# A gated encoder block: the recurrence's gate products as 64-row products in the two halves of the array

## The chip, the cores and the metric

The kernel runs on one core of a Trainium2 chip. The metric is the device time of one execution in microseconds (us), as the median of several runs. Profiles come from the hardware profiler; PE is TensorE, PEld its weight loads, DVE VectorE, ACT ScalarE, POOL GpSimd, SP the engine that issues the loads.

## The reference

One layer of a bidirectional encoder over 256 tokens of 1024 features, in fp32. Four mixers (a gated linear recurrence, differential attention, latent attention, retention) read one wide projection of the normalised input, are merged through sigmoid gates, and a feed-forward part follows. The change touches the recurrence alone:

```
xblk = xc.reshape(b, s, LRU_BLOCKS, LRU_BLOCK)        # 16 blocks of 64 features
for d in range(2):                                    # forwards and backwards in time
    r = sigmoid(einsum('bsnc,ncd->bsnd', xblk, wa[d]).reshape(b, s, w) + ba[d])
    i = sigmoid(einsum('bsnc,ncd->bsnd', xblk, wx[d]).reshape(b, s, w) + bx[d])
    log_a = -LRU_C * r * softplus(-lam[d])
    a = exp(log_a)
    u = sqrt(-expm1(2.0 * log_a)) * (i * xc)
    _, h = associative_scan(combine, (a, u), axis=1, reverse=(d == 1))
    h_sum = h_sum + h
return h_sum * gelu(ga)
```

The gates r and i are block-diagonal products: each block of 64 features is multiplied by a 64 × 64 matrix of its own, once for r and once for i, and for each direction d.

## The kernel before

The large products (`acc<-...` in the profile) stream weights from HBM. `load` fetches a tile `raw` of up to 1 MB (three buffers); `pieces` splits it into `hi` and `lo` (five buffers each), of which `hi` is written by ACT or, for some, by DVE, and `lo` by DVE; PE then makes three products in fp32r per piece. In `b_mode` 24 products of 256 columns use one piece, in `a_mode` 12 of up to 512.

The mixers run beside that stream as generators: `tick` after each weight tile advances those in the list `side`, by a credit that `pace` sets, and `finish` drains them. A scheduler then orders the instructions of each engine; every engine runs its own list in order. Nothing waits by time, only on semaphores. Loads of weights are given a higher priority than what stands around them.

The recurrence is made of 4 units u of 256 features. `a_in(u)` makes `xc`, with features on partitions: half f holds 128 features, that is two blocks of 64. `a_mix(u, xc, rr)` then makes the gates. Its weights come packed by `_pack_lru`: for each f, gate y and direction d a 128 × 128 matrix `bd` that holds two 64 × 64 blocks on its diagonal and zeros elsewhere. For each d there are four fp32 products of 128 rows (2 gates × 2 halves f), each with 256 columns (tokens), into two PSUM tiles `mm` (one per gate). ACT applies the sigmoid with the bias from the columns of `par` and writes `rr` (the r gate) and `ii` (the i gate). Later steps read them: ACT makes `aa` with Exp and Tanh of `rr`, DVE multiplies `ii` by `xc`, and a scan follows. `a_out(u)` needs the result, after the b mixer's projections.

On SP, the loads of `raw` and `bd` stand in one queue in order. POOL makes only the rsqrt steps (two instructions on a tile of a few columns each: `brs`, `bss`, `csc` and the like), whose readers are on DVE. Small tiles such as `rr`, `ii`, `aa`, `bd` and the copies `bx` of the b mixer are taken in turn from a pool `SH` of 16 buffers, so a new tile waits until the buffer's last reader is done.

Of the kernel before, what the change touches and what calls it, by code (L numbers as in the profile page):

```python
# [10 lines left out]
AF = mybir.ActivationFunctionType  # L11
# [62 lines left out]
def _pack_weights(w):  # L74
# [4 lines left out]
    for o, (name, r0, rows, n0, nn, mode) in offs.values():  # L79
# [3 lines left out]
        else:  # L83
# [2 lines left out]
    return flat  # L86


_COLS = (('norm1_g', 8), ('conv_w', 32), ('conv_b', 8), ('lru_ba', 16), ('lru_bx', 16),
         ('mla_qa_g', 3), ('mla_kva_g', 2), ('norm2_g', 8), ('norm3_g', 8), ('diff_sub_g', 1),  # L90
         ('ret_gn_g', 1), ('mla_q_g', 1), ('mla_k_g', 1), ('diff_q_g', 1), ('diff_k_g', 1),
         ('lru_lambda', 16))
# [11 lines left out]
def _pack_params(w):  # L104

    import numpy as np

    out = np.empty((P, N_PAR), np.float32)
    for name, k in _COLS:
        v = np.asarray(w[name][0])  # L110
        if name in ('diff_q_g', 'diff_k_g'):
            v = np.concatenate([np.ones(16, np.float32), v[16:]] * 2)
        elif name in ('mla_q_g', 'mla_k_g'):
            v = v[:P]
        out[:, _COL[name]:_COL[name] + k] = v.reshape(k, P).T
    rows = []
    for dn, mn in (('diff_q_g', 'mla_q_g'), ('diff_k_g', 'mla_k_g')):
        d, m = np.asarray(w[dn][0])[:16], np.asarray(w[mn][0])[P:]
        rows += [d, m, d[8:], d[:8], m[32:], m[:32]]
    rows.append(np.asarray(w['diff_lam'][0]).reshape(-1))  # L120
    out[:, O_GR:O_ROPE] = np.concatenate(rows)[None, :]
    out[:, O_ROPE:] = _rope().reshape(2, P, 288).transpose(1, 0, 2).reshape(P, 576)
    return out


def _pack_lru(w):

    import numpy as np

    out = np.zeros((4, 2, P, 2, 2, P), np.float32)  # L130
    for y, name in enumerate(('lru_wa', 'lru_wx')):
        v = np.asarray(w[name][0]).reshape(2, 4, 2, 2, 64, 64)
        for e in range(2):
            out[:, :, 64 * e:64 * e + 64, y, :, 64 * e:64 * e + 64] = v[:, :, :, e].transpose(1, 0, 3, 2, 4)
    return out


# [30 lines left out]
def encoder_kernel(ctx: ExitStack, tc: tile.TileContext, a, out):  # L168
# [17 lines left out]
    def mm_bank():  # L186
        return psmm.tile([P, 512], F32, tag="mm", name="mm")
# [7 lines left out]
    def act(o, x, f, **kw):  # L195
        nc.scalar.activation(o, x, f, **kw)  # L196

    def mm(o, lhsT, rhs, start, stop):
        nc.tensor.matmul(o, lhsT=lhsT, rhs=rhs, start=start, stop=stop)  # L199
# [246 lines left out]
    with tc.tile_pool(name="br", bufs=1) as br:  # L446
# [4 lines left out]
        def SH(name):  # L451
            return br.tile([P, 512], F32, tag="SH", name=name, bufs=NS)
# [66 lines left out]
        def a_mix(u, xc, rr):  # L519

            R, I, A = [], [], []
            bds = []
            for d in range(2):
                bd = SH("bd")
                nc.sync.dma_start(bd, a['lru'][u, d].rearrange("p y f n -> p (y f n)"))
                bds.append(bd.rearrange("p (y f n) -> p y f n", y=2, n=P))
            yield 0.1
            for d in range(2):
                bd = bds[d]
                R.append(rr if d == 0 else SH("rr").rearrange("p (f s) -> p f s", s=S))  # L530
                I.append(SH("ii").rearrange("p (f s) -> p f s", s=S))
                for y, (dst, bn) in enumerate(((R[d], 'lru_ba'), (I[d], 'lru_bx'))):
                    ps = mm_bank().rearrange("p (f s) -> p f s", s=S)
                    for f in range(2):
                        mm(ps[:, f, :], bd[:, y, f, :], xc[:, f, :], True, True)
                    for f in range(2):
                        act(dst[:, f, :], ps[:, f, :], AF.Sigmoid, bias=c1(bn, 8 * d + 2 * u + f))
                yield 1.5
            for d in range(2):
                A.append(SH("aa").rearrange("p (f s) -> p f s", s=S))  # L540
                aa, r_, i_ = A[d], R[d], I[d]
                for f in range(2):
                    c = 8 * d + 2 * u + f
                    act(aa[:, f, :], r_[:, f, :], AF.Exp, scale=sp[:, 1, c:c + 1])
                    act(r_[:, f, :], r_[:, f, :], AF.Tanh, scale=sp[:, 0, c:c + 1])
                sq = SH("sq").rearrange("p (f s) -> p f s", s=S)
                act(sq, aa, AF.Square)
                stt(r_, sq, 1.0, r_, ADD, MULT)
                tt(i_, i_, xc, MULT)
                yield 2.1  # L550
            for d in range(2):
                aa, r_, i_ = A[d], R[d], I[d]
                act(r_, r_, AF.Sqrt, bias=eps[:, 1:2])
                tt(i_, i_, r_, MULT)
                first = 0 if d == 0 else S - 1
                nc.vector.memset(aa[:, :, first:first + 1], 0.0)
                ao, uo, ho = (x.rearrange("p f s -> p (f s)") for x in (aa, i_, r_))
                if d == 1:
                    ao, uo, ho = ao[:, ::-1], uo[:, ::-1], ho[:, ::-1]
                nc.vector.tensor_tensor_scan(out=ho, data0=ao, data1=uo, initial=0.0, op0=MULT, op1=ADD)  # L560
                yield 1.8
            tt(R[0], R[0], R[1], ADD)
            yield 0.6
# [533 lines left out]
```

## Time and profile before

| what | value |
|---|---|
| three timed runs | 733.2, 734.09, 734.31 us; median 734.09 |
| the profiled execution | 732.92 us |
| its span | 731.1 us |
| granted clock of TensorE | full (1.0) |
| first and last gate product | 30.8 and 104.6 us from the span's start |
| DMA, mean over the span | 176 GB/s |

The span is the time between the first and the last instruction that the profiler saw. A timeline's row gives the start, the duration, the engine, the line, the operation, out<-in with partitions × elements, how many instructions were merged, and in square brackets how long the engine sat idle before and what released it. Durations of products overlap, since PE is pipelined: their cost is read from one start to the next. An fp32 product shows as two records. A row of the view of windows has the busy time of PE, PEld, DVE, ACT and POOL in this order, each with a count. In the views of DMAs, the last number is the median time from issue to landing.

### The profile page before, as it was taken

The page shows a single profiled execution, that of the slowest core. Times are in us where ns is not written, and L with a number is a line of the kernel's source. Part 1 is how long each engine was busy: PE and PEld are TensorE (multiplying, and loading weights), DVE is VectorE, ACT ScalarE, POOL GpSimd, SP SyncE. Part 2 cuts the span into 40 slices and gives each one's busy share as a digit, 9 for nine tenths or more (in the row PEclk, how much of TensorE's full clock was granted, in tenths as well). Part 3 has the DMA queues.
Part 4 walks back from the last instruction along what each step waited for, and adds up shares of the span by engine and source line. Part 5 has one row for each costly group of instructions (what it writes and reads, how often), then busy time and mean ns, then how long its engine had stood idle before and what let it go on. Part 6 is the DMA issues. An engine that isn't in the chain of part 4 may idle for free.

```text
span 731.1 us, 10616 instructions
## 1 busy us (share of the span) xinstructions
PE 714.7 (98%) x4066; PEld 622.6 (85%) x4066; DVE 526.2 (72%) x893; ACT 427.7 (58%) x744; POOL 49.3 (7%) x58
## 2 busy tenths in 40 slices
PE   5999999999999999999999999999999999999997
PEld 4988889997888898888888888878899999888886
DVE  5988978998777879976775788576666666446652
ACT  7589867483755996556654443545755555445551
POOL 0000012222011033110000101000000000000000
PEclk9999999999999999999999999999999999999999
DMA  8754544365344254444545475553565555636611
GB/s 312 260 212 173 172 173 145 114 248 182 134 162 137 91 177 169 173 159 144 179 166 217 138 256 197 191 184 143 177 225 176 173 177 185 215 118 229 233 53 58
DMA packets 22802, 128.47 MB, mean 176 GB/s; under 512 B 2656, under 2 KB 2912, under 8 KB 9440
## 3 DMA queue, kind: packets, MB, share of 16 engines
q1 hardware_dynamic: 22752, 127.80, 49.8%
q8 instruction: 32, 0.52, 0.3%
q14 instruction: 18, 0.15, 0.1%
HBM read 126.74 MB, written 1.05 MB: 175 GB/s over the span
## 4 chain that ended last, share of the span: by engine, by line
PE 64%; DVE 1%; ACT 0%; issue 0%
PE acc L199 57%; PE mm L199 3%; PE mm L212 2%; PE mm L203 1%; ACT hi L196 0%; DVE lo L190 0%; DVE gate L193 0%; DVE pg L190 0%; DVE y L193 0%; DVE xs L190 0%; ACT pg L196 0%
## 5 line engine op out<-in xcount | busy, mean ns | idle before, releaser
L190 DVE TENSOR_TENSOR lo<-raw,hi 128x1024 fp32r<-128x1024 f32 (+3 forms) x226 | 268.2, 1192 | 116.6 <-ACT hi L196 116.0
L196 ACT ACTIVATE hi<-raw 128x1024 fp32r<-128x1024 f32 (+2 forms) x200 | 207.7, 1043 | 192.6 <-PE acc L199 161.2
L199 PE MATMUL acc<-hi,xTh 128*128 128x512 f32 (+3 forms) x376 | 146.3, 389 | 0.0
L199 PE MATMUL acc<-hi,xTl 128*128 128x512 f32 (+3 forms) x376 | 142.8, 380 | 0.0
L199 PE MATMUL acc<-lo,xTh 128*128 128x512 f32 (+3 forms) x376 | 142.5, 379 | 0.0
L199 PE MATMUL acc<-hi,y 128*128 128x512 f32 x448 | 142.1, 393 | 0.0
L199 PE MATMUL acc<-xTl,hi 128*128 128x256 f32 x384 | 109.2, 285 | 0.2 <-DVE xTl L193 0.2
L199 PE MATMUL acc<-xTh,hi 128*128 128x256 f32 x384 | 109.2, 286 | 0.0
L199 PE MATMUL acc<-xTh,lo 128*128 128x256 f32 x384 | 108.7, 284 | 0.0
L199 PEld LDWEIGHTS acc<-hi,y 128*128 128x128 f32 x448 | 84.1, 188 | 17.5
L199 PE MATMUL acc<-lo,y 128*128 128x512 f32 x224 | 87.8, 392 | 0.0
L199 PEld LDWEIGHTS acc<-hi,xTl 128*128 128x128 f32 x376 | 70.6, 188 | 13.2
L199 PEld LDWEIGHTS acc<-hi,xTh 128*128 128x128 f32 x376 | 70.7, 188 | 12.9
L199 PEld LDWEIGHTS acc<-lo,xTh 128*128 128x128 f32 x376 | 70.8, 188 | 12.2
L199 PEld LDWEIGHTS acc<-xTl,hi 128*128 128x128 f32 x384 | 74.1, 193 | 0.7 <-DVE xTl L193 0.6
L199 PEld LDWEIGHTS acc<-xTh,hi 128*128 128x128 f32 x384 | 73.9, 193 | 0.1
L199 PEld LDWEIGHTS acc<-xTh,lo 128*128 128x128 f32 x384 | 73.8, 193 | 0.1
L199 PEld LDWEIGHTS acc<-lo,y 128*128 128x128 f32 x224 | 42.1, 188 | 8.3
L199 PE MATMUL acc<-hi,h 128*128 128x512 f32 x128 | 40.8, 398 | 0.0
L199 PEld LDWEIGHTS acc<-hi,h 128*128 128x128 f32 x128 | 24.0, 188 | 5.7
L199 PE MATMUL acc<-lo,h 128*128 128x512 f32 x64 | 25.3, 396 | 0.0
L199 PE MATMUL acc<-hi,cT 128*128 128x384 f32 (+1 forms) x80 | 24.2, 369 | 0.8 <-ACT cqp L196 0.8
(225 smaller groups left out, 889.9 us busy)
## 6 DMA issues: line engine op xcount, KB each, us to landing
raw<-in_weights_dram SPq DMA_DIRECT2D x104, 1024.0 KB, 4.8
raw<-in_weights_dram SPq DMA_DIRECT2D x6, 512.0 KB, 3.5
raw<-in_weights_dram SPq DMA_DIRECT2D x4, 576.0 KB, 3.8
bd<-in_lru_dram SPq DMA_DIRECT2D x8, 256.0 KB, 5.3
gb<-in_gate_b_dram SPq DMA_DIRECT2D x8, 256.0 KB, 5.2
dec<-in_decay_dram SPq DMA_DIRECT2D x8, 256.0 KB, 6.2
raw<-in_weights_dram SPq DMA_DIRECT2D x2, 768.0 KB, 4.3
raw<-in_weights_dram SPq DMA_DIRECT2D x2, 640.0 KB, 3.7
```

What stands on the lines that cost most here:

```text
L190: nc.vector.tensor_tensor(out=o, in0=x, in1=y, op=op)
L196: nc.scalar.activation(o, x, f, **kw)
L199: nc.tensor.matmul(o, lhsT=lhsT, rhs=rhs, start=start, stop=stop)
L203: nc.tensor.matmul(o, lhsT=lhsT, rhs=rhs, start=start, stop=stop, skip_group_check=True)
L212: nc.tensor.transpose(o, x, ident[:x.shape[0], :x.shape[0]])
```

## The change

Each gate product of 128 rows becomes two of 64 rows. `_pack_lru` no longer writes block-diagonal matrices with zeros: for each block of 64 features it puts the r matrix in columns 0 to 63 and the i matrix in columns 64 to 127. Block e = 0 lies on partitions 0 to 63 and e = 1 on partitions 64 to 127, each with its own PSUM tile, so the products of one half f use the upper and the lower half of the array in turn. The number of products is the same: 4 per direction and unit. The weights of both directions now fit one tile `bd` of 256 KB; before there were two.

After the sigmoids, the tile `g[0]` holds r of block 0 on partitions 0 to 63 and i of block 0 on partitions 64 to 127; `g[1]` (named `gx`) holds the same of block 1. Three DMAs on POOL's queue put the halves where the rest of the code reads them. The biases are packed to match.

```
-_COLS = (('norm1_g', 8), ('conv_w', 32), ('conv_b', 8), ('lru_ba', 16), ('lru_bx', 16),
+_COLS = (('norm1_g', 8), ('conv_w', 32), ('conv_b', 8), ('lru_b', 32),
...
+        if name == 'lru_b':
+            v = np.concatenate([np.asarray(w[n][0]).reshape(32, 64) for n in ('lru_ba', 'lru_bx')], axis=1)
...
-    out = np.zeros((4, 2, P, 2, 2, P), np.float32)
+    out = np.zeros((4, P, 2, 2, P), np.float32)
...
-            out[:, :, 64 * e:64 * e + 64, y, :, 64 * e:64 * e + 64] = v[:, :, :, e].transpose(1, 0, 3, 2, 4)
+            out[:, 64 * e:64 * e + 64, :, :, 64 * y:64 * y + 64] = v[:, :, :, e].transpose(1, 3, 0, 2, 4)
...
         def a_mix(u, xc, rr):
             R, I, A = [], [], []
-            bds = []
+            bd = SH("bd")
+            nc.sync.dma_start(bd, a['lru'][u].rearrange("p d f n -> p (d f n)"))
+            bd = bd.rearrange("p (d f n) -> p d f n", d=2, n=P)
+            yield 0.1
             for d in range(2):
-                bd = SH("bd")
-                nc.sync.dma_start(bd, a['lru'][u, d].rearrange("p y f n -> p (y f n)"))
-                bds.append(bd.rearrange("p (y f n) -> p y f n", y=2, n=P))
-            yield 0.1
-            for d in range(2):
-                bd = bds[d]
-                R.append(rr if d == 0 else SH("rr").rearrange("p (f s) -> p f s", s=S))
-                I.append(SH("ii").rearrange("p (f s) -> p f s", s=S))
-                for y, (dst, bn) in enumerate(((R[d], 'lru_ba'), (I[d], 'lru_bx'))):
-                    ps = mm_bank().rearrange("p (f s) -> p f s", s=S)
+                ps = [mm_bank().rearrange("p (f s) -> p f s", s=S) for _ in range(2)]
+                for f in range(2):
+                    for e in range(2):
+                        w = slice(64 * e, 64 * e + 64)
+                        mm(ps[e][:, f, :], bd[w, d, f, :], xc[w, f, :], True, True)
+                g = [rr if d == 0 else SH("rr"), SH("gx")]
+                g = [x.rearrange("p (f s) -> p f s", s=S) if len(x.shape) == 2 else x for x in g]
+                for e in range(2):
                     for f in range(2):
-                        mm(ps[:, f, :], bd[:, y, f, :], xc[:, f, :], True, True)
-                    for f in range(2):
-                        act(dst[:, f, :], ps[:, f, :], AF.Sigmoid, bias=c1(bn, 8 * d + 2 * u + f))
+                        act(g[e][:, f, :], ps[e][:, f, :], AF.Sigmoid, bias=c1('lru_b', 2 * (8 * d + 2 * u + f) + e))
+                ii = SH("ii").rearrange("p (f s) -> p f s", s=S)
+                nc.gpsimd.dma_start(ii[0:64], g[0][64:128])
+                nc.gpsimd.dma_start(ii[64:128], g[1][64:128])
+                nc.gpsimd.dma_start(g[0][64:128], g[1][0:64])
+                R.append(g[0])
+                I.append(ii)
                 yield 1.5
```

The scheduler moves other instructions with it. On PE, at the second group of gate products (u = 0, second direction, and u = 1, first direction), `mm<-xc,bd` stood in one run of eight:

```order
L199 MATMUL acc<-xTl,hi 128x256
L199 MATMUL acc<-xTh,lo 128x256
L199 MATMUL mm<-xc,bd 128x256 x8
L199 MATMUL acc<-hi,xTh 128x512
L199 MATMUL acc<-lo,xTh 128x512
```

Now it stands, in the changed kernel, with its own line numbers:

```order
L203 MATMUL acc<-xTl,hi 128x256
L203 MATMUL acc<-xTh,lo 128x256
L203 MATMUL mm<-xc,bd 128x256 x4
L203 MATMUL acc<-hi,xTh 128x512
L203 MATMUL mm<-xc,bd 128x256 x4
L203 MATMUL acc<-lo,xTh 128x512
```

One ordinary product moved between the two directions. The other groups stand where they stood: one of 4 ahead of this place, and behind it one of 8 and three of 4.

On SP, at the loads for u = 1 (`bd_409` and `bd_411` before, one for each direction; the numbers tell tiles apart), the queue was:

```order
L371 DMA raw_424<-in_weights_dram 128x2048
L371 DMA raw_524<-in_weights_dram 128x2048
L371 DMA raw_594<-in_weights_dram 128x2048
L371 DMA raw_660<-in_weights_dram 128x2048
L525 DMA bd_409<-in_lru_dram 128x512
L525 DMA bd_411<-in_lru_dram 128x512
L371 DMA raw_707<-in_weights_dram 128x2048
```

and in the changed kernel, from the same `raw_424` on, with one `bd_411` for both directions:

```order
L375 DMA raw_424<-in_weights_dram 128x2048
L375 DMA raw_530<-in_weights_dram 128x2048
L375 DMA raw_606<-in_weights_dram 128x2048
L375 DMA raw_672<-in_weights_dram 128x2048
L375 DMA raw_719<-in_weights_dram 128x2048
L527 DMA bd_411<-in_lru_dram 128x512
L375 DMA raw_771<-in_weights_dram 128x2048
```

The load of `bd` for u = 1 moved behind a fifth weight load.

On POOL, which had nothing but rsqrt steps there, this is the end of the swaps in the changed kernel (u = 3; `rr_1071`, `gx_1072` and `ii_1077` belong to its second direction, `brs` to the b mixer), with the engines that an instruction waits for in brackets:

```order
L544 DMA ii_1026<-rr_523 64x512 [waits DMASW2_49,DVE_49,DMAHW1_49,PE_49,Activation_49]
L545 DMA ii_1026<-gx_1021 64x512 [waits Activation_49]
L546 DMA rr_523<-gx_1021 64x512 [waits DMASW4_49,DMASW2_49]
L544 DMA ii_1077<-rr_1071 64x512 [waits DMASW5_49,DVE_49,Activation_49]
L545 DMA ii_1077<-gx_1072 64x512 [waits DMASW6_49,Activation_49]
L299 TENSOR_SCALAR brs_663<-brs_663 128x8 [waits DVE_49]
L300 TENSOR_TENSOR brs_663<-brs_663,nhalf_95 128x8 [waits Pool_49]
L546 DMA rr_1071<-gx_1072 64x512 [waits DMASW5_49,DMASW1_49,DMASW0_49]
L299 TENSOR_SCALAR brs_669<-brs_669 128x8 [waits DVE_49]
```

The last swap of a set waits for the first one's landing (DMASW), since it overwrites what that one reads; for u = 3 it stands behind the first rsqrt pair. Two more places in the new order matter further on: on ACT, the first copies `bx<-acc` of the b mixer wait for the last swap of u = 1's second direction, since they reuse a buffer that it reads; and on DVE, near the multiply `bx<-bx,brs` that waits for POOL, one more `lo`, a `bT` and a `gel` now stand ahead of that multiply. ACT has 19 table loads in place of 18.

More of the change, by code (lines that the diff above doesn't have):

```diff
@@ L109, in _pack_params @@
     for name, k in _COLS:
-        v = np.asarray(w[name][0])
+        if name == 'lru_b':
+            v = np.concatenate([np.asarray(w[n][0]).reshape(32, 64) for n in ('lru_ba', 'lru_bx')], axis=1)
+        else:
+            v = np.asarray(w[name][0])
         if name in ('diff_q_g', 'diff_k_g'):
```

## The prediction, made before the changed kernel ran

> **What bounds the kernel now.** I read the page first: the share of each engine, then the chain of waits.
>
> ```profile
> span 731.1 us, 10616 instructions
> PE 714.7 (98%) x4066; PEld 622.6 (85%) x4066; DVE 526.2 (72%) x893; ACT 427.7 (58%) x744; POOL 49.3 (7%) x58
> PE acc L199 57%; PE mm L199 3%; PE mm L212 2%; PE mm L203 1%; ACT hi L196 0%; DVE lo L190 0%; DVE gate L193 0%; DVE pg L190 0%; DVE y L193 0%; DVE xs L190 0%; ACT pg L196 0%
> ```
>
> PE is busy for 98% of the span, and the chain that ended last is PE's own products. The view of PE's waits says where it is not busy:
>
> ```profile
> PE mm L212 <- DVE nst L190: 7.5, 1, 7.5
> PE mm L212 <- DVE cT L193: 1.4, 1, 1.4
> ```
>
> 7.5 us are the start, which the change leaves alone. The 1.4 us are one stop at 181 us, well behind the gates (they end at 106 us). So time taken out of PE's stream between 30 and 105 us comes off the end, **as long as** the pieces hi and lo and the chain to 181 us keep up with a PE that is early.
>
> **The gate products before.** The view of the tile bd, then PE's timeline (start, duration, what) around the first group:
>
> ```profile
> L199 PE MATMUL mm<-xc,bd x64: 377/379/380, 30.8 to 104.6; 128*128 128x256 f32 x64
> ...
> 30.53 0.28 PE L199 MATMUL acc<-xTl,hi 128*128 128x256 f32 x1
> 30.65 0.28 PE L199 MATMUL acc<-xTh,lo 128*128 128x256 f32 x1
> 30.77 1.89 PE L199 MATMUL mm<-xc,bd 128*128 128x256 f32 x8
> 32.31 0.47 PE L199 MATMUL acc<-xTh,hi 128*128 128x256 f32 x1
> 32.62 0.28 PE L199 MATMUL acc<-xTl,hi 128*128 128x256 f32 x1
> 32.73 0.29 PE L199 MATMUL acc<-xTh,lo 128*128 128x256 f32 x1
> ```
>
> Durations overlap, so I go by starts. The 32 products leave 64 records: fp32 runs as two passes. From 30.65 to 32.62 is 1.97 us; two steps of an ordinary product (30.53 to 30.65, 0.12 each) go off, and 8 passes take 1.73 us, 0.216 each, with nothing lost at either end. All 64: **13.8 us**.
>
> **What 64-row products cost.** The kernel already has such products, in fp32r: attention scores of 12 and of 24.
>
> ```profile
> 148.56 0.33 PE L199 MATMUL acc<-lo,xTh 128*128 128x384 f32 x1
> 148.74 0.34 PE L199 MATMUL acc<-hi,xTl 128*128 128x384 f32 x1
> 149.00 0.98 PE L199 MATMUL mm<-bT 64*128 64x256 f32 x12
> 149.91 0.42 PE L199 MATMUL acc<-hi,xTh 128*128 128x320 f32 x1
> 150.16 0.31 PE L199 MATMUL acc<-lo,xTh 128*128 128x320 f32 x1
> 150.31 0.31 PE L199 MATMUL acc<-hi,xTl 128*128 128x320 f32 x1
> ...
> 393.20 0.39 PE L199 MATMUL acc<-lo,xTh 128*128 128x512 f32 x1
> 393.43 0.39 PE L199 MATMUL acc<-hi,xTl 128*128 128x512 f32 x1
> 393.75 1.69 PE L199 MATMUL mm<-dqk 64*128 64x256 f32 x24
> 395.37 0.50 PE L199 MATMUL acc<-hi,xTh 128*128 128x512 f32 x1
> 395.70 0.39 PE L199 MATMUL acc<-lo,xTh 128*128 128x512 f32 x1
> ```
>
> Twelve: 148.74 to 150.16 is 1.42, less the neighbours' steps (0.18 and 0.15), 1.09 us. Twenty-four: 393.43 to 395.70 is 2.27, less 0.23 twice, 1.81 us. Twelve more cost 0.72, so a pair in the two halves costs 0.12, as much as one 128-row product of 256 columns: the halves run at the same time. What is left, 1.09 less 0.72, is a fixed **0.4 us per block**, paid on going into and out of 64-row products.
>
> **The change, term by term.**
>
> 1. PE. 32 products of 128 rows become 32 of 64 rows, 64 passes again, now 32 pairs. In the new order they stand in seven blocks, six of 4 products and one of 8; where 16 records ran in one piece before, an ordinary product now parts two of the blocks. No row shows fp32 in 64 rows. Bounds: pairs fully side by side, 32 times 0.216 = 6.9 us, or no overlap, 13.8 us; to each come 7 times 0.4 = 2.8. That is 9.7 or 16.6 against 13.8: **4.1 us less, or 2.8 more**. I take 4.1, by the nearest rows, bT and dqk.
>
> A rule of the Trainium skill speaks against that: "TensorE: Matmul & The Clock Gate", section "The mechanism", says that products start and end strictly in program order. The two passes of a product use the same half, so in strict order only the second pass of one could overlap the first of the next. But bT is issued three products on one half, then three on the other, which in strict order would be 9 steps of 0.12 for its 12 and not the 6 that it takes; the trace does not agree with that rule. It is a rival below all the same.
>
> 2. SP. The load of bd for u = 1 now stands behind one more load of raw than before:
>
> ```profile
> 33.88 5.52 SPq L371 DMA_DIRECT2D raw<-in_weights_dram  x2
> raw<-in_weights_dram SPq DMA_DIRECT2D x104, 1024.0 KB, 4.8
> bd<-in_lru_dram SPq DMA_DIRECT2D x8, 256.0 KB, 5.3
> 38.25 3.62 PE L199 MATMUL mm<-xc,bd 128*128 128x256 f32 x16
> ```
>
> That raw went out at 33.88, so bd goes at about 34.3 and lands 5.3 later, at 39.6. PE would want it at 38.25 less 0.5 already won, plus one block (0.4 + 4 × 0.216 = 1.3) and one product, 39.2. I charge **0.5 us**, bounds 0 and 1. Only half the bd loads are left, at the same size each.
>
> 3. The swaps. Each of 8 gate sets adds three DMAs of 128 KB on POOL's queue: two that put i together from both tiles, and one that fills the upper half of r. The third waits for the first to land, so r is whole two landings after its sigmoids. Call one landing, issue included, L. No row shows a DMA from POOL or within SBUF. The nearest rows are bd above, of the same row length, 5.3 us, behind a weight load in its own queue; and 128 KB at the quiet end:
>
> ```profile
> out_dram<-pg SPq DMA_DIRECT2D x2, 128.0 KB, 1.7
> ```
>
> I take the middle, L = 3.5, and keep 1.7 and 5.3 as ends. The Trainium skill has a price for a DMA that POOL issues, "DMA: Bandwidth & Descriptors", section "Anatomy of one DMA": about 2.0 us plus bytes at 436 GB/s. By it L would be an estimated 2.3, and the sum below would not change; no run here shows it.
>
> What waits for them: the sigmoids' readers, on ACT and DVE in order, with the pieces hi and lo queued behind them. The place with the least room early on is one lo at 62.5 us:
>
> ```profile
> 49.75 0.84 ACT L196 ACTIVATE rr<-mm,par 128x256 f32<-128x256 f32 x2
> 60.38 1.16 ACT L196 ACTIVATE bx<-acc 128x256 f32<-128x256 f32 x4
> 62.52 2.36 DVE L190 TENSOR_TENSOR lo<-raw,hi 128x1024 fp32r<-128x1024 f32 x2 [0.71 <-ACT hi L196]
> 67.20 0.39 PE L199 MATMUL acc<-lo,xTh 128*128 128x512 f32 x1
> ```
>
> In the new order the copies bx wait on ACT for the last swap of u = 1, as it had read a buffer that they reuse. Its r is done at 50.6, so bx starts at 50.6 + 2L or later. The first lo of that row is done about 3.4 us after bx starts (60.38 to 63.75), at 54.0 + 2L. PE wants it at 67.2 less 2.3 won by then: **no stop up to L = 5.4**, then 2 us per us.
>
> The other place is u = 3. Its last swap stands on POOL behind a pair of rsqrt instructions (order of POOL):
>
> ```profile
> 107.64 1.66 POOL L296 TENSOR_TENSOR brs<-brs,nhalf 128x8 f32<-128x8 f32 x1
> 104.29 0.82 ACT L196 ACTIVATE rr<-mm,par 128x256 f32<-128x256 f32 x2
> 111.01 0.90 ACT L196 ACTIVATE aa<-rr,sp 128x256 f32<-128x256 f32 x2
> 113.26 0.69 DVE L193 SCALAR_TENSOR_TENSOR rr<-sq,rr 128x512 f32<-128x512 f32 x1 [1.42 <-ACT sq L196]
> 137.44 0.69 DVE L190 TENSOR_TENSOR bx<-bx,brs 128x512 f32<-128x512 f32 x1 [1.81 <-POOL brs L296]
> 150.00:170.00 20.00, 20.00 (x121) 17.89 (x122) 19.26 (x48) 13.37 (x34) 5.14 (x5) 1.00 0.63 230
> 181.56 0.44 PE L212 MATMUL mm<-ident,cs 128*128 128x128 f32 x2 [1.42 <-DVE cT L193]
> ```
>
> All times here move with PE's lead. The swap goes out at 109.3 and lands L later, or 2L after 105.1 where that is more; the Exp that needs it stood at 111.0. So it is late by L − 1.7, above L = 4.2 by 2L − 5.9. Behind it DVE has next to no gaps (busy 19.26 of the 20 us from 150 to 170, the third busy figure of that row), so a delay would travel to PE's stop at 181.56. One gap is on the way, 1.81 us at 137.4, where bx waits for POOL; in the new order another lo, bT and gel stand ahead of that bx and fill it. **Longer stop: L − 3.5**, above 4.2 it is 2L − 7.7; at L = 3.5 nothing.
>
> 4. At no cost: sigmoids, multiplies and scans are as many as before. ACT gets one more table load, behind the hi for that tight lo; the ring of five pieces covers it. If it did not, it would be
>
> ```profile
> 30.36 1.28 ACT L196 ACT_TABLE_LOAD   x1
> ```
>
> **Sum.** −4.1 + 0.5 + 0 = −3.6 us. The profiled execution took 732.92 us, so 729.3 on its scale. The three timed runs were 733.2 to 734.31, median 734.09, that is 1.2 above it; I put the median of the changed kernel between the two scales, at **730.0**.
>
> **Rivals.** A: the forecast, halves side by side and swaps in time, 0.57.
>
> B: strict order. A block of 4 takes 5 steps of 0.216 and 0.4, 1.48 us; the block of 8 takes 9, 2.34; together 11.2. The gain is 2.6 in place of 4.1, and the time 731.5. Against it stand the twelve bT products; for it, that no fp32 pass has been seen in halves. 0.10.
>
> C: late swaps. One mechanism, the landing time: at L = 5 the stop at 181 us grows by 2.3 and 1.3 of the gain is left, 732.3. At 5.5 the added stops (3.3 and 0.2) have eaten the 3.6. At L = 6.5 they are 5.3 and 2.2, 3.9 more than the gain, 737.5: **slower**. For it speaks bd at 5.3 and that POOL builds each transfer itself; against it, that bd's 5.3 is mostly the weight load ahead of it and that a swap is half as large. 0.15 for about no change, 0.10 for slower.
>
> D: the change does not do what it says, fp32 halves run one after another: 2.8 and 0.5 more, 737.3. Against it bT and dqk. 0.08.
>
> **How the numbers follow.** This kernel's measurement can tell about 0.2%, 1.5 us, from no change. Faster takes A and B, 0.67; within it the middle of C, 0.15; slower the rest of C and D, 0.18. The low end of the range is A with bd in time and the 1.4 us stop at 181 gone as well (L = 1.7): 730.0 − 0.5 − 1.4 = 728.1, and 0.6 for the two scales, 727.5. The high end takes in the part of C that cancels or passes the gain up to L of about 6, 735.5; beyond it lie 0.1 or so of C and D.
>
> **What would show it.** bd's tile view should show 64 passes as 64*128, in pairs that start within hundredths of a us, and a block of four spanning about 1.3 us between its neighbours. If the passes start 0.216 apart one by one, D; if every other one overlaps, B. The swaps' landing times on POOL's queue settle L; ACT's waits for the swaps at bx and at the last aa, and the length of PE's stop on cT, settle C. A PE wait on bd near 39 us is the 0.5. What would make it wrong is a landing over 5 us, or a switch to 64 rows that costs fp32 more than 0.4.

## The result and the profile after

The changed kernel took 743.04 us (median of 4, 741.58 to 743.82), the kernel before, on the same chip, 733.86 (733.2 to 734.31): 1.0122 times as long, 95% interval 1.0109 to 1.0134. The prediction, 730.0 with a range up to 735.5, has the wrong sign. Of its rivals C came true, late swaps, by more than it was priced.

From the page of the changed kernel, the span and the engines:

```profile
span 741.2 us, 10685 instructions
PE 714.0 (96%) x4066; PEld 617.0 (83%) x4066; DVE 526.0 (71%) x893; ACT 429.1 (58%) x745; POOL 67.3 (9%) x82
```

The span is 10.1 us longer, and PE is busy for 96% of it in place of 98%: it waits more. (Its busy time is only 0.7 us less, though the gate products alone were to take 4.1 off; part of the reason comes below.) Lines have moved by four: L203 is the product that was L199, L200 ACT, L194 DVE's two-tensor operations. PE's waits (engine, line, releaser: us in all, times, the longest):

```profile
PE mm L216 <- DVE nst L194: 8.4, 1, 8.4
PE mm L216 <- DVE bx L194: 4.7, 3, 2.6
PE acc L203 <- DVE lo L194: 2.4, 3, 1.2
PE mm L203 <- DMA bd<-in_lru_dram: 1.8, 1, 1.8
PE acc L203 <- ACT hi L200: 1.1, 1, 1.1
PE mm L216 <- DVE cT L197: 1.1, 1, 1.1
```

Before there were two lines here, 7.5 and 1.4. Four are new, 10.0 us in all. One of them, on bd, is the gate products' wait for their weights; the others come behind the gate products, which themselves are as fast as forecast. The view of bd:

```profile
L203 PE MATMUL mm<-xc,bd x64: 375/376/481, 31.8 to 107.1; 64*128 64x256 f32 x64
```

and PE's timeline around the first block (start, duration, what):

```profile
31.56 0.28 PE L203 MATMUL acc<-xTh,lo 128*128 128x256 f32 x1
31.77 1.13 PE L203 MATMUL mm<-xc,bd 64*128 64x256 f32 x8
...
33.06 0.28 PE L203 MATMUL acc<-xTl,hi 128*128 128x256 f32 x1
```

From 31.56 to 33.06 is 1.50 us; two steps of 0.12 go off, 1.26 are left for a block that took 1.73 before. Priced were 4 × 0.216 + 0.4 = 1.26.

So what do bx, lo and hi wait for? The DMA view has the swaps' landing times (KB each, median us from issue to landing):

```profile
bd<-in_lru_dram SPq DMA_DIRECT2D x4, 256.0 KB, 7.7
ii<-rr POOLq DMA_DIRECT2D x8, 128.0 KB, 3.5
ii<-gx POOLq DMA_DIRECT2D x8, 128.0 KB, 4.6
rr<-gx POOLq DMA_DIRECT2D x8, 128.0 KB, 5.2
```

The first median is the very 3.5 that the prediction took for all. It is the middle of two things. The same view for what is issued between 46 and 52 us:

```profile
rr<-gx POOLq DMA_DIRECT2D x2, 128.0 KB, 2.3
```

and between 57.85 and 60.2, where a weight load goes out:

```profile
raw<-in_weights_dram SPq DMA_DIRECT2D x1, 1024.0 KB, 6.9
rr<-gx POOLq DMA_DIRECT2D x2, 128.0 KB, 6.8
...
ii<-gx POOLq DMA_DIRECT2D x1, 128.0 KB, 7.1
```

The trace's records of single transfers around 58, 89 and 111 us, issue and landing:

```
56.02 -> 58.36   2.3  POOL ii<-rr
56.74 -> 59.02   2.3  POOL ii<-gx
57.47 -> 59.73   2.3  POOL ii<-rr
57.88 -> 64.78   6.9  SP   raw
58.20 -> 65.28   7.1  POOL ii<-gx
58.71 -> 65.89   7.2  POOL rr<-gx
60.01 -> 66.46   6.4  POOL rr<-gx

83.08 -> 88.51   5.4  SP   raw
83.52 -> 89.02   5.5  POOL ii<-rr

111.12 -> 119.11  8.0  SP   raw
111.52 -> 118.59  7.1  POOL ii<-gx
115.31 -> 122.51  7.2  SP   raw
116.75 -> 122.74  6.0  POOL rr<-gx
```

A swap issued while no weight load is on its way, or one in its last microsecond, lands in 2.2 to 2.7 us; that holds for 9 of the 24. The other 15 went out with a load on its way that had 3 us or more to go. They took 3.9 to 7.8 us, though they stand in another queue: 11 of them landed within 1.2 us of a load that was on its way, the other four 1.7 to 3.4 us behind it. The load of 57.88 gets longer as well, 6.9 us in place of 4.8 (those of 111.12 and 115.31, with 8.0 and 7.2, also met another load).

Who reads the late swaps, and who stands behind the readers? DVE and ACT in the changed kernel, at two places (in brackets: idle before, released by):

```profile
65.36 0.69 DVE L194 TENSOR_TENSOR ii<-ii,xc 128x512 f32<-128x512 f32 x1 [5.56 <-DMA ii<-gx]
...
118.68 0.69 DVE L194 TENSOR_TENSOR ii<-ii,xc 128x512 f32<-128x512 f32 x1 [3.43 <-DMA ii<-gx]
...
119.88 0.29 DVE L194 TENSOR_TENSOR bx<-ropea,ropeb 128x128 f32<-128x128 f32 x1
...
125.08 0.69 DVE L197 SCALAR_TENSOR_TENSOR rr<-sq,rr 128x512 f32<-128x512 f32 x1 [3.69 <-ACT sq L200]
```

```profile
65.99 1.36 ACT L200 ACTIVATE bx<-acc 128x256 f32<-128x256 f32 x4 [2.42 <-DMA rr<-gx]
67.23 1.06 ACT L200 ACTIVATE hi<-raw 128x1024 fp32r<-128x1024 f32 x1
...
122.83 0.91 ACT L200 ACTIVATE aa<-rr,sp 128x256 f32<-128x256 f32 x2 [4.82 <-DMA rr<-gx]
```

and PE behind them:

```profile
68.35 0.50 PE L203 MATMUL acc<-hi,xTh 128*128 128x512 f32 x1 [1.14 <-ACT hi L200]
69.61 0.50 PE L203 MATMUL acc<-lo,xTh 128*128 128x512 f32 x1 [0.76 <-DVE lo L194]
...
120.32 0.63 PE L216 MATMUL mm<-ident,bx 128*128 128x128 f32 x4 [1.76 <-DVE bx L194]
...
153.23 0.94 PE L216 MATMUL mm<-ident,bx 128*128 128x128 f32 x4 [2.62 <-DVE bx L194]
```

Read from the right: the swap issued at 58.71 lands at 65.89; at 65.99 ACT, which had idled 2.42 us, copies bx (into a buffer that this swap read), then cuts hi at 67.23; PE has waited 1.14 us for it when it starts at 68.35. And the swap of 111.52 lands at 118.59, DVE's product with xc follows at 118.68, three short operations on, bx is whole at 120.17, and PE transposes it at 120.32, 1.76 late.

POOL shows the other half of the chain at 111 to 123 us:

```profile
113.49 0.56 POOL L299 TENSOR_SCALAR brs<-brs 128x8 f32<-128x8 f32 x1 [1.46 <-DVE brs L634]
114.13 2.65 POOL L300 TENSOR_TENSOR brs<-brs,nhalf 128x8 f32<-128x8 f32 x1
116.75 0.60 POOL L546 DMA_DIRECT2D rr<-gx  x1
```

The last swap of u = 3 goes out only behind the rsqrt pair, at 116.75. It lands at 122.74; ACT makes aa and then sq from it, and DVE, which idles 3.69 us for sq, goes on at 125.08. From there to 153 us DVE idles for less than 1 us in all, so what it lost at 118 and 125 us travels along it: this is the third stop on bx, the longest, 2.62 us at 153.23.

The stops are not the whole loss. With 10.0 us of new stops and 4 us won, some 4 of the 10.1 us are left; 0.9 of them are the start (8.4 in place of 7.5). Another part is a stretch at half the clock, which follows the stop at 153 us. The view of windows has the granted clock behind the counts of the engines, then the DMA share and GB/s:

```profile
153.50:156.90 3.40, 3.40 (x14) 3.40 (x13) 3.40 (x9) 1.10 (x3) 2.34 (x2) 0.50 0.81 282
```

At a clock of 0.50 the products of 384 columns start 0.32 us apart, where they started 0.17 apart before and after it, and PE falls 1.4 us further behind. About 2 us more were not taken apart. Of the 16 traces of this case nine have such a stretch, of 3.4 to 10.2 us at a time, in the middle of the kernel. They are the nine in which PE, once it had started, stood still for 2.0 us or more at one stop; in the other seven the longest stop is 1.5. Not every such stop is followed by one, and the cause was not tested.

### The profile page after: what moved, and what is told of

Its sections match the earlier page's. It is cut to its first block, busy times and chain, and to the rows that moved or that the text cites. A ratio compares the mean times of both kernels' runs of the same rounds, so it can differ in the third digit from the quotient of the medians.

```text
span 741.2 us, 10685 instructions
## 1 busy us (share of the span) xinstructions
PE 714.0 (96%) x4066; PEld 617.0 (83%) x4066; DVE 526.0 (71%) x893; ACT 429.1 (58%) x745; POOL 67.3 (9%) x82
## 4 chain that ended last, share of the span: by engine, by line
PE 63%; DVE 1%; ACT 0%; issue 0%
PE acc L203 57%; PE mm L203 3%; PE mm L216 2%; PE mm L207 1%; ACT hi L200 0%; DVE lo L194 0%; DVE gate L197 0%; DVE pg L194 0%; DVE y L197 0%; DVE xs L194 0%; ACT pg L200 0%
## 5 line engine op out<-in xcount | busy, mean ns | idle before, releaser
L194 DVE TENSOR_TENSOR lo<-raw,hi 128x1024 fp32r<-128x1024 f32 (+3 forms) x226 | 268.2, 1192 | 115.0 <-ACT hi L200 114.5
L200 ACT ACTIVATE hi<-raw 128x1024 fp32r<-128x1024 f32 (+2 forms) x200 | 207.5, 1043 | 184.9 <-PE acc L203 152.0
L203 PE MATMUL acc<-hi,xTh 128*128 128x512 f32 (+3 forms) x376 | 146.7, 390 | 1.1 <-ACT hi L200 1.1
L203 PE MATMUL acc<-lo,xTh 128*128 128x512 f32 (+3 forms) x376 | 143.5, 382 | 2.0 <-DVE lo L194 2.0
L203 PE MATMUL acc<-hi,xTl 128*128 128x512 f32 (+3 forms) x376 | 143.3, 381 | 0.0
L203 PE MATMUL acc<-hi,y 128*128 128x512 f32 x448 | 142.1, 393 | 0.0
L203 PE MATMUL acc<-xTl,hi 128*128 128x256 f32 x384 | 109.0, 284 | 0.2 <-DVE xTl L197 0.2
L203 PE MATMUL acc<-xTh,hi 128*128 128x256 f32 x384 | 108.9, 285 | 0.2 <-ACT xTh L200 0.2
L203 PE MATMUL acc<-xTh,lo 128*128 128x256 f32 x384 | 108.7, 284 | 0.4 <-DVE lo L194 0.4
L203 PEld LDWEIGHTS acc<-hi,y 128*128 128x128 f32 x448 | 84.1, 188 | 17.5
L203 PE MATMUL acc<-lo,y 128*128 128x512 f32 x224 | 87.8, 392 | 0.0
L203 PEld LDWEIGHTS acc<-hi,xTh 128*128 128x128 f32 x376 | 71.3, 190 | 16.1 <-ACT hi L200 1.9
L203 PEld LDWEIGHTS acc<-lo,xTh 128*128 128x128 f32 x376 | 71.2, 189 | 15.0 <-DVE lo L194 2.6
L203 PEld LDWEIGHTS acc<-hi,xTl 128*128 128x128 f32 x376 | 71.1, 189 | 13.1
L203 PEld LDWEIGHTS acc<-xTl,hi 128*128 128x128 f32 x384 | 73.8, 192 | 0.7 <-DVE xTl L197 0.5
L203 PEld LDWEIGHTS acc<-xTh,hi 128*128 128x128 f32 x384 | 73.6, 192 | 0.8 <-ACT xTh L200 0.4
L203 PEld LDWEIGHTS acc<-xTh,lo 128*128 128x128 f32 x384 | 73.6, 192 | 0.7 <-DVE lo L194 0.6
L203 PEld LDWEIGHTS acc<-lo,y 128*128 128x128 f32 x224 | 42.1, 188 | 8.3
L203 PE MATMUL acc<-hi,h 128*128 128x512 f32 x128 | 40.8, 398 | 0.0
L203 PEld LDWEIGHTS acc<-hi,h 128*128 128x128 f32 x128 | 24.0, 188 | 5.7
L203 PE MATMUL acc<-lo,h 128*128 128x512 f32 x64 | 25.3, 396 | 0.0
```

The lines of the kernel that those rows point to most:

```text
L194: nc.vector.tensor_tensor(out=o, in0=x, in1=y, op=op)
```

## The experiments

Theory S: the products win what was priced; the swaps lose it several times over, since they land behind weight loads and since their readers stand in order ahead of hi, lo and bx. Against it: the 64-row products or their new order are what costs (P); POOL's issuing or the two halves of the partitions make swaps slow (Q); their bytes do (B); the late bd does (D). All runs, each beside the kernel before on its chip (medians 733.4 to 733.9):

| kernel | us, median and range | ratio to before, 95% interval |
|---|---|---|
| the change | 743.04, 741.58 to 743.82 | 1.0109 to 1.0134 |
| no swaps | 729.24, 729.19 to 731.36 | 0.9935 to 0.9965 |
| swaps with 128-row products | 741.29, 738.02 to 741.80 | 1.0071 to 1.0124 |
| small swaps | 739.49, 736.75 to 740.32 | 1.0056 to 1.0097 |
| copies on POOL | 727.89, 727.50 to 730.45 | 0.9915 to 0.9950 |
| no weight loads, 34 to 123 us | 733.19, 729.76 to 735.50 | 0.9968 to 1.0004 |
| weight loads in quarters | 748.23, 747.14 to 749.16 | 1.0178 to 1.0211 |
| bd early | 742.26, 740.96 to 745.05 | 1.0096 to 1.0150 |
| sigmoids by halves on ACT | 739.46, 739.09 to 739.82 | 1.0060 to 1.0090 |
| four swaps, one landing | 738.63, 738.29 to 738.96 | 1.0052 to 1.0082 |
| readers later | 748.19, 746.87 to 748.77 | 1.0180 to 1.0210 |
| copies on DVE | 729.84, 729.42 to 730.92 | 0.9936 to 0.9969 |
| copies on POOL, bd early | 727.74, 727.23 to 728.22 | 0.9904 to 0.9934 |
| no weight loads, four swaps | 733.56, 732.61 to 736.20 | 0.9989 to 1.0009 |
| no weight loads, bd early | 731.81, 730.56 to 732.46 | 0.9959 to 0.9984 |

Where the time goes can be followed with one measure: the start of the n-th product into a tile acc (counted from 0) less its start before, from the traces (us):

| n (start before) | the change | no swaps | 128 rows, swaps | small swaps | POOL copies | no loads |
|---|---|---|---|---|---|---|
| 100 (25.5) | 0.9 | 0.0 | 0.6 | 0.4 | −0.1 | 0.6 |
| 217 (50.9) | 0.0 | −2.1 | 0.6 | −2.0 | −2.7 | −1.0 |
| 312 (74.0) | 2.2 | −2.4 | 3.0 | −2.4 | −3.0 | 0.8 |
| 480 (116.1) | 4.6 | −3.5 | 3.0 | 5.6 | −4.0 | −0.3 |
| 540 (123.4) | 5.2 | −3.5 | 3.0 | 7.3 | −4.0 | −0.3 |
| 700 (145.4) | 9.8 | −3.5 | 8.0 | 7.3 | −4.0 | 0.3 |
| 900 (196.4) | 10.2 | −4.5 | 8.2 | 6.4 | −5.0 | 1.5 |
| 3000 (652.5) | 10.2 | −4.4 | 8.3 | 6.4 | −5.0 | 1.6 |

The first row is ahead of the gates. The up to 0.9 there come and go from run to run: "copies on POOL, bd early" has 0.4 in it, "sigmoids by halves", which has no swap either, 0.9. Stretches at half clock are in the rows 540 (small swaps, 118.9 to 125.7 us) and 700 (the change; 128 rows, 150.8 to 154.2).

### No swaps

```diff
-                ii = SH("ii").rearrange("p (f s) -> p f s", s=S)
-                nc.gpsimd.dma_start(ii[0:64], g[0][64:128])
-                nc.gpsimd.dma_start(ii[64:128], g[1][64:128])
-                nc.gpsimd.dma_start(g[0][64:128], g[1][0:64])
...
-                I.append(ii)
+                I.append(g[1])
```

> The changed kernel without the three swaps of each gate set: the products in the halves, the order of the sigmoids and the load of bd stay, the recurrence reads the tiles as the sigmoids left them, so the halves of r and i are mixed up and the recurrence's numbers are others. Theory S (the side-by-side products win what the prediction priced, 4.1 us, and the swaps lose about 13 us because they land late behind weight loads): 729 to 732.5 us, of which bd's stop of 1.8 us near 40 us stays. Rival P (the 64-row products, their order or the shorter load of bd lose the time, the swaps nothing): 740 to 744 us.

729.24: as S has it. PE's waits there show no bd, bx, lo or hi; at 40 us 0.5 us are left, for xc:

```profile
PE mm L203 <- ACT xc L200: 0.5, 1, 0.5
PE mm L216 <- DVE cT L197: 0.5, 1, 0.5
```

P falls. The swaps cost 743.0 − 729.2 = 13.8 us, with all that follows from them, the half clock too.

### Swaps with 128-row products

```diff
+    out = np.zeros((4, 2, P, 2, 2, P), np.float32)
...
+            out[:, :, 64 * e:64 * e + 64, e, :, 64 * y:64 * y + 64] = v[:, :, :, e].transpose(1, 0, 3, 2, 4)
...
+                for e in range(2):
+                    for f in range(2):
+                        mm(ps[e][:, f, :], bds[d][:, e, f, :], xc[:, f, :], True, True)
```

> The changed kernel with its products put back: the block matrices are padded with zeros again, so that each of the 32 products has 128 rows and fills the same PSUM rows as now; the swaps stay as they are, bd is again two loads. Theory S: the time of before, 733.9, plus what the swaps cost, 12 to 14 us: 745 to 748 us. Rival P: 733 to 736 us.

741.29, 7.9 us over before: P falls again, but S's range was missed by 3.7 us. The two parts don't add: alone the products win 4.2 and the swaps lose 7.9, together they lose 9.2. PE's waits:

```profile
PE mm L216 <- DVE bx L194: 3.8, 1, 3.8
PE acc L203 <- ACT hi L200: 1.1, 1, 1.1
```

With 0.8 for lo the new stops are 5.7 us here, against 10.0 in the change: where PE waits for swaps, the swaps set its time, and a PE that is 4 us early waits 4 us longer. Under the swaps, the products' gain can't be seen: the intervals of this kernel and of the change overlap.

### Small swaps

```diff
+                nc.gpsimd.dma_start(g[1][64:128, 0, 0:16], g[0][64:128, 0, 0:16])
+                nc.gpsimd.dma_start(g[1][0:64, 0, 16:32], g[0][0:64, 0, 16:32])
+                nc.gpsimd.dma_start(g[0][64:128, 0, 0:16], g[1][0:64, 0, 0:16])
...
+                I.append(g[1])
```

> The changed kernel with swaps of the same number, queue, partitions and waits, but 64 bytes of each row in place of 2048 (4 KB a swap, not 128): most of r and i stays unswapped, so the recurrence's numbers are others. Theory S1 (a swap waits in the DMA engines behind the weight load under way, whatever its size): landings stay at 4 to 7 us where a weight load is under way, 738 to 743 us. Rival B (its own bytes make a swap slow): landings of 2 to 2.5 us everywhere, 729 to 733 us.

739.49, inside S1's range (S1 is the part of S that says that a swap waits behind the load, whatever its size). The DMA view:

```profile
gx<-rr POOLq DMA_DIRECT2D x16, 4.0 KB, 3.4
rr<-gx POOLq DMA_DIRECT2D x8, 4.0 KB, 3.6
```

A thirty-second of the bytes, and landings are still 1.6 to 2.0 us alone and 3.5 to 6.2 behind a load (four lie between, of 2.3 to 3.0, three of them issued in a load's last 2.2 us): one 4 KB swap went out at 55.52, 0.06 after a load, and landed at 60.31, 0.19 after that load. What the DMA engines did meanwhile is in the view of their packets; from 56.40 to 59.45 it has, on any queue, only these (packets, MB, share, which counts packets that run on behind the window too):

```profile
q1 hardware_dynamic: 128, 1.05, 103.4%
```

These are the load's own 128 packets of 8 KB. Three small swaps had been issued, at 55.52, 56.03 and 56.88, and all of their packets start behind the load's last one, from 59.53 on. Size has a part early on (by the 312th product nothing is lost), but of the 13.8 us 10.3 stay. Most of them come at one place:

```profile
PE mm L216 <- DVE bx L194: 7.4, 1, 7.4
```

There a small swap lands at 109.35 behind a load, DVE's product that reads it starts at 109.47 and sets the sum of squares for rsqrt back, rsqrt on POOL sets the last swap back to 114.12, and that lands behind the next load, at 117.58. The stretch at half clock around it costs 1.7 us more, the step from 5.6 to 7.3 in the table.

### Copies on POOL

```diff
-                nc.gpsimd.dma_start(ii[0:64], g[0][64:128])
+                nc.gpsimd.tensor_copy(ii[0:64], g[0][64:128])
```

and so for the other two.

> The changed kernel with each swap made by a copy on POOL (64x512 from one half of the partitions to the other) in place of a DMA; same result. Theory S: if a copy takes 1 us or so there is no wait for a DMA engine, r and i are whole about 3 us after the sigmoids, and the products' gain stays: 729 to 733 us. If a copy takes 2 us or more, the third is done over 6 us after the sigmoids, as late as the swaps now: 736 to 743 us. Rival P: 740 us or more either way.

727.89, faster than both kernels: 0.9932 of before, interval 0.9915 to 0.9950. POOL's groups (x count, busy us, mean ns):

```profile
L544 POOL COPY ii<-rr 64x512 f32<-64x512 f32 x8 | 9.4, 1174 | 76.7 <-ACT rr L200 76.6
L546 POOL COPY rr<-gx 64x512 f32<-64x512 f32 x8 | 9.3, 1164 | 0.5
L545 POOL COPY ii<-gx 64x512 f32<-64x512 f32 x8 | 7.6, 945 | 0.5
```

26 us on an engine that stood idle, about 1.1 us a copy. In the table above the gain grows with the blocks of gate products to 4.0 us, and 1.0 us more comes at the stop for cT, which is 0.5 there. It is the best of the study, with bd early (below) as good.

### No weight loads from 34 to 123 us

```diff
+        nload[0] += 1
+        if 8 <= nload[0] <= 20:
...
+            return nload[1]
         raw = raws.tile([P, 2048], F32, tag="raw", name="raw", bufs=3)
+        nload[1] = raw
```

> The changed kernel, swaps and all, but without the 13 weight loads that fall between 34 and 123 us (the 8th to the 20th): the pieces hi and lo of that stretch are cut from the 7th load again, so the products there use other weights. Theory S1 (a swap waits behind the weight load under way): every swap lands in 2 to 3 us, the stops go, and the products' gain is seen: 727 to 731 us. Rival Q (POOL's queue, the two halves of the partitions or the swaps' own crowd make them slow): landings of 4 us and more stay, 738 to 743 us.

Behind 57 us the swaps land as S1 says; of those issued from there on, by the DMA view of that stretch:

```profile
ii<-rr POOLq DMA_DIRECT2D x5, 128.0 KB, 2.2
ii<-gx POOLq DMA_DIRECT2D x5, 128.0 KB, 2.2
rr<-gx POOLq DMA_DIRECT2D x5, 128.0 KB, 2.2
```

The same stretch of the changed kernel has 4.7, 5.2 and 6.0. Q falls: POOL, the halves and the crowd are the same here. The time, 733.19, is 10 us less than with the loads, but above the 727 to 731 expected, and it spreads over 5.7 us. Seven of the nine swaps before 57 us still took 3.9 to 7.6 us: two later loads had moved up to 34 and 38 us, and a load of bd went out at 46.49, beside them.

### The rest: one landing, and an early bd, with and without loads

Four swaps for three, r into a tile of its own:

```diff
+                g = [SH("gr"), SH("gx"), rr if d == 0 else SH("rr")]
...
-                nc.gpsimd.dma_start(g[0][64:128], g[1][0:64])
+                nc.gpsimd.dma_start(g[2][64:128], g[1][0:64])
+                nc.gpsimd.dma_start(g[2][0:64], g[0][0:64])
```

> The changed kernel with four swaps a set in place of three: r goes whole into a tile of its own, lower half from one sigmoid tile and upper half from the other, so no swap waits for another to land, and for u = 3 all four go out ahead of the rsqrt pair on POOL. Same result. Theory S2 (the second landing and the place behind rsqrt make a good part of the loss): 735 to 740 us, and the late swap at 116.75 us goes. Rival L (the landing behind a weight load is nearly all, one or two of them alike): 741 to 746 us, since a third more swaps crowd the DMA engines.

738.63, 4.4 us less than the change, inside the range for S2, the theory named above. On POOL the last swaps of u = 3 now stand ahead of rsqrt:

```profile
110.08 0.52 POOL L547 DMA_DIRECT2D rr<-gr  x1
114.82 0.56 POOL L299 TENSOR_SCALAR brs<-brs 128x8 f32<-128x8 f32 x1 [4.22 <-DVE brs L635]
```

One landing in place of two takes away a third of what the swaps cost, though the engines carry a third more swaps.

The load of bd one group earlier:

```diff
+            for v in range(u if u == 0 else u + 1, min(u + 2, 4)):
+                bds[v] = SH("bd")
+                nc.sync.dma_start(bds[v], a['lru'][v].rearrange("p d f n -> p (d f n)"))
```

> The changed kernel with the load of bd issued one group earlier (for u = 1 beside that for u = 0), swaps kept; same result. The stop of 1.8 us near 40 us goes. Theory S: the later stops behind the swaps take up most of what that wins, as they are set by when the swaps land: 741 to 743 us. Rival D (the late bd is the cause, and everything behind it follows): 733 to 738 us.

742.26: PE's stop on bd is gone, and the time stays; the intervals overlap. D falls. The later stops take up what the early one gives.

Both edits were then made in the kernel without the 13 loads.

> The kernel without the 8th to the 20th weight load (its products there use other weights), with three swaps a set and the load of bd one group earlier. If the rest of 4 us is bd, which lands late there behind a load that has moved up (a stop of 1.3 us), and what follows from it: 730 to 732 us. If not: 733 us or more.

> The kernel without the 8th to the 20th weight load (its products there use other weights) and with four swaps a set in place of three, so that none waits for another to land. The kernel without those loads took 733.2 us, 4 more than the one without swaps. If that rest is the second landing and the place behind rsqrt on POOL: 729 to 731 us. If it is something else: 732 to 734 us.

Without loads the early bd does show, 731.81, 1.4 less than 733.19, about the stop of 1.3 us that it removes. One landing in place of two does not, 733.56. But this does not show that the second landing costs nothing without a load: in the trace of that kernel (736.2 us, the slowest of its ten runs) the stop on cT is 1.0 us shorter, and a new one of 2.0 us, on hi at 69 us, has 6.8 us at half clock with it. With the early bd, what is left of the 4 us over the kernel without swaps, 2.6, lies in short stops (lo 0.8, be 0.8, cT 1.5 in place of 0.5) and was not taken apart further.

### Weight loads in quarters

```diff
+            n = 4 if 7 <= nload[0] <= 20 else 1
+            for q in range(n):
+                w = slice(q * sz // n, (q + 1) * sz // n)
+                nc.sync.dma_start(raw[:, w], src[:, w])
```

> The changed kernel with each of the 14 weight loads from the 7th to the 20th issued as four DMAs of a quarter of each row (2 KB of 8); same result. If the DMA engines take up what was queued first and finish it, a swap still waits for all four quarters: landings of 4 to 8 us where a load is under way, 739 to 744 us. If they take turns between the queues piece by piece, smaller pieces let the swaps through: landings of 2.5 to 4 us, 730 to 737 us.

748.23, slower still, above both ranges:

```profile
raw<-in_weights_dram SPq DMA_DIRECT2D x56, 256.0 KB, 4.9
ii<-rr POOLq DMA_DIRECT2D x8, 128.0 KB, 5.1
ii<-gx POOLq DMA_DIRECT2D x8, 128.0 KB, 6.2
rr<-gx POOLq DMA_DIRECT2D x8, 128.0 KB, 5.3
```

Smaller pieces don't let the swaps through: their landings are longer, and a quarter takes as long as a whole load did. One swap went out at 55.84, behind four quarters (53.72 to 55.05) and a bd (55.59). The view of packets from 54.60 to 59.75 has none on POOL's queue:

```profile
q1 hardware_dynamic: 602, 1.11, 79.7%
```

545 of them have 2 KB, more than the 512 of the four quarters; the swap's first packet starts at 59.76. Part of the time is the clock again: with a stop of 5.6 us, on hi, go 10.2 us at half.

### Readers later

```diff
-                yield 1.5
+                yield 1.5 if d == 0 else 6.0
```

> The changed kernel with the readers of r and i (Exp on ACT, the product with xc on DVE) written later: the step that holds both gate sets is given 6.0 in place of 1.5 units of pace, so more of hi, lo and bx stands ahead of the readers on ACT and DVE. Swaps, bytes and result stay. Theory S (a late landing costs because its readers stand in order ahead of hi, lo and bx): landings stay at 4 to 7 us but the stops shrink, 731 to 740 us. Rival: the stops come from the landings whatever stands behind the readers, 741 us or more.

748.19: as a remedy it failed, and S's range was missed. The first part went as S says: swaps land no sooner (medians 5.4, 5.9 and 4.7 us), and yet at the 312th product PE is 4.0 us ahead of before, where the change is 2.2 behind. But the recurrence slips into the stretch of the Gelu, where ACT loads a table, 1.28 us each time, seven times between 132 and 150 us, and hi comes late:

```profile
151.00 1.01 PE L203 MATMUL acc<-hi,xTh 128*128 128x384 f32 x2 [8.03 <-ACT hi L200]
```

A stretch of 10.2 us at half clock goes with it. By the 900th product PE is 8.9 us behind, by the 3000th 15.4; where the last 6.5 were lost was not taken apart.

### Two other ways to do without swaps

Sigmoids by halves, each written straight to the partitions where r and i belong:

```diff
+                for y, t_ in enumerate((r_, ii)):
+                    for f in range(2):
+                        for e in range(2):
+                            h = slice(64 * y, 64 * y + 64)
+                            j = _COL['lru_b'] + 2 * (8 * d + 2 * u + f) + e
+                            act(t_[64 * e:64 * e + 64, f, :], ps[e][h, f, :], AF.Sigmoid, bias=par[h, j:j + 1])
```

> The changed kernel without swaps and with the same result: each sigmoid of 128 rows becomes two of 64 rows, which write r and i straight into the partitions where they belong, so 64 ACT instructions in place of 32. If one of 64 rows takes 0.42 us as one of 128 does, ACT has 13 us more between 30 and 125 us. Theory S: no DMA is waited for, the gain stays if ACT's time is covered: 727 to 732 us. If ACT's time is not covered, hi comes late by some us: 733 to 738 us.

739.46. A sigmoid of 64 rows takes as long as one of 128 (x count, busy us, mean ns; the last line is the changed kernel's):

```profile
L200 ACT ACTIVATE ii<-mm,par 64x256 f32<-64x256 f32 x32 | 15.1, 471 | 0.5
L200 ACT ACTIVATE rr<-mm,par 64x256 f32<-64x256 f32 x32 | 14.6, 468 | 0.5
...
L200 ACT ACTIVATE rr<-mm,par 128x256 f32<-128x256 f32 x16 | 6.8, 475 | 0.2
```

30 us of ACT for what took 13.6, and hi is late by 3.3 us in all.

> The copies of the kernel with POOL copies made on DVE instead; same result. DVE has 24 copies more, 0.3 to 0.7 us each, 7 to 17 us between 35 and 120 us, in order with lo and bx. If DVE's gaps cover them: 727 to 731 us; if not, lo comes late: 731 to 738 us.

729.84: DVE has room for the copies too. Whether a little less than POOL is not shown, as the intervals overlap.

> POOL copies in place of swaps, and the load of bd one group earlier; same result. In the kernel with POOL copies PE had no stop on bd, so the earlier load has nothing to win: 727 to 729 us, within 0.2% of that kernel. If moving a block of gate products ahead of one ordinary product merges two blocks of 64 rows, 0.4 us less.

727.74, the same as with the later bd: where nothing collides, bd has nothing to give. Two blocks of gate products did merge; the 0.4 us for that are not seen in the times, but from the 100th to the 480th product PE wins 4.5 us here and 3.9 with the later bd.

## Why the prediction was wrong, point by point

1. **The products: right.** A block of four takes 1.26 us, as priced, and by the 480th product, behind all blocks, the kernel with POOL copies is 4.0 us ahead (priced 4.1). That is not rival B's 1.48 a block, nor D.

2. **bd: near alone, and partly by luck; wrong among swaps.** 0.5 us were charged; without swaps 0.5 are left there, but for xc, and with copies on POOL nothing is. With swaps bd lands after 6.8 us, where it took 5.5 without them, and PE waits 1.8. It hardly mattered: taking it away won nothing that can be told from the spread.

3. **The swaps: the step that failed is the choice of L = 3.5**, with its reason that bd's 5.3 us is "mostly the weight load ahead of it and that a swap is half as large". The row was read rightly; the conclusion was not. bd and raw stand in one queue, and the text took it that a swap in POOL's queue does not stand behind the load. It does: 2.2 to 2.7 us without a load, 3.9 to 7.8 with one, and 4 KB wait like 128. The two ends of the range for L were two cases, not the bounds of one; none of the 24 landings lies between 2.7 and 3.8. What had to be counted was how many swaps go out during a load, and 15 of 24 did. By the Trainium skill, "DMA: Bandwidth & Descriptors", section "Anatomy of one DMA", a swap was an estimated 2.3 us; the trace agrees where nothing else is on the way, and only there. By the Trainium skill, "DMA: Bandwidth & Descriptors", section "Queues, rings and completion order", each DMA engine goes round its queues and changes over only at the end of a packet, typically of 9 to 17 descriptors. That is another packet than the profile's: if each of the 128 packets of 8 KB that the view has for a load is one descriptor, the load is, as an estimate from that figure, about one such packet on each of 16 engines, and a swap behind it waits for all of it; the landing 0.19 us behind the load agrees. With loads in quarters the swaps did not get through either; how the engines put those together, no run shows.

4. **What a late swap costs: right in kind, too small.** The chain named for u = 3 (behind rsqrt on POOL) is there, and so is the early one (bx behind the last swap of u = 1). With L = 7, about what those swaps took (7.2; 7.1 and 6.0), the prediction's own terms give 2 × 7 − 10.8 = 3.2 and 2 × 7 − 7.7 = 6.3 us of stops, 739.5 in all. Measured are 1.9 at the first place and, at the second, bx's 4.7 in three stops; cT's stop did not grow (1.1): the waiting came ahead of it. That it came as bx at 153 us and not as cT at 181 is what the prediction had wrong of the path. Not priced were lo's 1.2 at 100 us, behind the last swap of u = 2's second direction, the extra 1.3 for bd, and the half clock behind the stop at 153 us, 1.4.

5. **The rest at no cost: right.** Without the swaps PE's only new wait up to 200 us is 0.5 us for xc. The chance for "slower" through C, 0.10, rested on landings over 5.5 us all through; late ones at the two tight places were enough.

## What to carry to other kernels

A small DMA inside this kernel, which streams weights, had two prices, one with a load on its way and one without, and a queue of its own did not change that: count how many fall into a load, and look what stands in order behind each reader. To move data between halves of the partitions where an engine is idle, copy there: 1.1 us for 64x512 on POOL, without meeting the loads. And a gain on the bounding engine is worth nothing while another chain sets its time: the 4 us that the products win without swaps could not be seen with them.

## What the runs showed of the hardware that was not expected

A 4 KB transfer landed with the 1 MB load issued 0.06 us before it on another queue: none of its packets started before all 128 of the load had. PE's granted clock was 0.50 for 3.4 to 10.2 us at a time in the nine kernels with a stop of 2.0 us or more, and in none of the seven without. Fp32 products of 64 rows in two halves run side by side as fp32r ones do, 0.216 us for a pair of passes and, by the block measured, 0.4 more for a block. A copy of 64x512 on POOL takes from 0.6 to 2.4 us in one run; why was not tried.
